# Down-projection products of 512 columns cut into pairs of 256, but for 56 of 240

## The chip, the cores and the metric

The kernel runs on one core of one Trainium2 chip. Its time is the device time of one execution in microseconds, and of several executions the median. TensorE (PE in the profile) does matrix products, VectorE (DVE) and ScalarE (ACT) elementwise work, GpSimd (POOL) odd pieces; SyncE (SP) issues most of the transfers between HBM and SBUF, the memory on the core. PE writes its sums into PSUM, whose banks hold 512 float32 columns each.

## The reference

One decoder layer on 256 tokens of 1024 channels: two mixing branches (a recurrent one and an attention one), merged and projected, and then a gated feed-forward part with a causal convolution of width 3. Only the last part is touched:

```python
def conv_ffn(h, w_up, conv_w, conv_b, w_down):        # h (1, 256, 1024), D_FF = 2816
    u = h @ w_up                                      # (1024, 5632)
    a, b = u[..., :D_FF], u[..., D_FF:]
    a = conv1d_causal(a, conv_w) + conv_b             # width 3, per channel
    return (gelu(a, approximate=False) * b) @ w_down  # (2816, 1024)
...
    x = x + conv_ffn(rms_norm(x, norm2_g), w_ffn_up, ffn_conv_w, ffn_conv_b, w_ffn_down)
```

## The kernel before

All matrix products run in a reduced float32 format. To keep accuracy, each operand is split into a high part and a low remainder (`whi` and `wlo` for weights; `hh`, `hl` and `hb[:, 0]`, `hb[:, 1]` for activations), and each product is done three times: high by high, low by high, high by low.

A product on PE has two operands. The stationary one, 128 by 128, is loaded first by an instruction of its own (PEld in the profile, LDWEIGHTS); then the moving one streams through it, 256 or 512 columns long, and the result is added into PSUM. Every product in this kernel has its own load, also when the tile is the same as before.

Weights come in groups of 1024 columns per partition (512 KB). `weights()` hands out the next group, already split, and has the next ones made ready: ScalarE copies the high part (`split_hi`, line 299), VectorE subtracts for the low part (`split_lo`, line 310), SyncE starts the next transfer (`load_next`). The order of the groups is one fixed queue.

The feed-forward part works in eleven blocks `j` of 256 hidden channels. For each block:

- `up()` computes the gate half into an `acc` bank and then, through `up(atp)`, the value half into an `at` bank. Both run `wst` (lines 346, 348, 351): the weights are stationary, the activations `hx` move, 256 columns (tokens) in each product. That is 2 x 48 = 96 products.
- VectorE and ScalarE scale, convolve and apply GELU, multiply with the value half and split the result into `hb`.
- `down(j, hb)` multiplies with two groups of down-projection weights (`i` = 0, 1), 128 hidden channels each. Here `hb` is stationary and the weights move. There are four sums `fin[f]`, each one bank of 512 columns: `t` is the half of the tokens, `hf` the half of the output channels. Three products each (lines 1464, 1466, 1468) make 2 x 4 x 3 = 24 products of 512 columns.

`down` runs one block behind: block `j`'s down-projection stands on PE after the up-projections of block `j` + 1. The last block's is written out by hand (lines 1513 to 1529): its sums 0 to 2 are done in products of 512 columns, and the last sum in two halves of 256 columns, so that they can be scaled and stored one after another.

Two earlier stages matter for comparison. In `queries` (lines 1322, 1323) one stationary tile serves two products in a row, one of 288 columns into `acc` and one of 256 into `pq`. In the output projection (`xst`, lines 367, 368, 371) `mh` and `ml` are stationary and 512 columns of weights move.

Of the kernel before, what the change touches and what calls it, by code (L numbers as in the profile page):

```python
# [37 lines left out]
def body(tc, x, positions, norm1_g, w_in, rwkv_mu, w_decay_up, decay_bias, w_aaa_up,  # L38
# [3 lines left out]
    act, dve, pool, pe = nc.scalar, nc.vector, nc.gpsimd, nc.tensor  # L42
    ctx = ExitStack()
    with ctx:
# [12 lines left out]
        def b4(name, shape=(128, 4, 256), dt=F32):  # L57
            return sb.tile(list(shape), dt, name=name, tag="b4", bufs=NB4)
# [14 lines left out]
        def chp(name="ch"):  # L73
            return ps.tile([128, 512], F32, name=name, tag="ch", bufs=3)

        def atp(name="at"):
            return ps.tile([128, 512], F32, name=name, tag="at", bufs=2)
# [243 lines left out]
        def weights(n=1):  # L321

            w = ready.pop(0)
            taken[0] += 1
            for _ in range(n):
                with tc.issue_after(fence[0]) if taken[0] < 6 else nullcontext():
                    split_lo()
                    split_hi()
            return w
# [1093 lines left out]
        for i, (c0, c1) in enumerate(zip(WCUT, WCUT[1:])):  # L1423
            cs = slice(c0, c1)
# [31 lines left out]
        def down(j, hb):  # L1456
            for i in range(2):
                wh, wl = weights()
                st = j == 0 and i == 0
                for f in range(4):  # L1460
                    t, hf = divmod(f, 2)
                    ts = slice(t * 128, t * 128 + 128)
                    cs = slice(hf * 512, hf * 512 + 512)
                    pe.matmul(fin[f], hb[:, 0, i, ts], wh[:, 0, cs], start=st, stop=False,  # L1464
                              skip_group_check=f == 3)
                    pe.matmul(fin[f], hb[:, 1, i, ts], wh[:, 0, cs], start=False, stop=False,  # L1466
                              skip_group_check=f == 3)
                    pe.matmul(fin[f], hb[:, 0, i, ts], wl[:, 0, cs], start=False, stop=False,  # L1468
                              skip_group_check=f == 3)

        prev = []
        for j in range(11):
            hb = b4("hb", (128, 2, 2, 256), F32R)
            if j == 0:
# [3 lines left out]
                fin = [chp("f0"), chp("f1"), chp("f2"), atp("f3")]  # L1478
# [5 lines left out]
            for m in range(2):  # L1484
                n = 2 * j + m
# [17 lines left out]
            if len(prev) == 2:  # L1503
                down(*prev.pop(0))
        of = out.rearrange("b s d -> (b s) d")
        j, hb = prev.pop(0)
# [6 lines left out]
        for f, is_ in ((0, (0,)), (1, (0,)), (0, (1,)), (2, (0,)), (1, (1,)), (2, (1,)), (3, (0, 1)), (4, (0, 1))):  # L1513
            t, hf = divmod(min(f, 3), 2)
            ts = slice(t * 128, t * 128 + 128)
            c0, n = ((0, 512), (0, 256), (256, 256))[max(f - 2, 0)]
            fs = last if f == 4 else fin[f][:, c0:c0 + n]
            cs = slice(hf * 512 + c0, hf * 512 + c0 + n)
            kw = dict(skip_group_check=True) if f == 3 else {}
            for i in is_:  # L1520
                wh, wl = ws[i]
# [32 lines left out]
```

## Time and profile before

| | us |
|---|---|
| median of 3 runs | 402.79 (402.75 to 403.62) |
| the profiled execution | 402.01 |
| its span, first to last instruction | 400.2 |
| PE busy in it | 394.3, 99% |
| VectorE busy | 301.9, 75% |
| ScalarE busy | 237.3, 59% |
| one block of the feed-forward part, from the second on | 16.40 |

Times are microseconds from the start of the span unless marked ns. An instruction's group is given by its line, engine, operation, the tile written and the tiles read (`f<-whi,hb` is `fin` from `whi` and `hb`), partitions by columns, and a count. The chain of waits is followed back from the last instruction to what released each step. Products on PE overlap: the end of one lies after the start of the next, so the distance between starts tells what one costs, and the listed duration does not.

### The profile page before, as it was taken

The numbers are of one execution on the slowest core, as the hardware profiler recorded it, in microseconds if no ns is written. First come the engines' busy times: TensorE is split into PE (matmuls) and PEld (weight loads), VectorE is DVE, ScalarE is ACT, GpSimd is POOL, SyncE is SP. The second block draws the span as 40 slices with busy tenths as digits, with TensorE's granted clock in tenths as the row PEclk, the third lists the DMA queues.
The fourth block names the chain that finished last, engine by engine and source line by source line (L and its number), as shares of the span: only waits on it lengthen the run. The fifth ranks groups of instructions, "written<-read, shape, count | busy, mean of one in ns | idle before, by whom it ended". The sixth has DMA issues, their size and how long they took to land.

```text
span 400.2 us, 9024 instructions
## 1 busy us (share of the span) xinstructions
PE 394.3 (99%) x3633; PEld 365.9 (91%) x3633; DVE 301.9 (75%) x508; ACT 237.3 (59%) x411; POOL 49.5 (12%) x87
## 2 busy tenths in 40 slices
PE   8999999999999999999999999999999999999996
PEld 6899999898999989999888999999999999999995
DVE  4989989899868989688875885765757667576583
ACT  5899477494747686635554874554545546455350
POOL 8888000010600021120000000000000000000000
PEclk9999999999999999999999999999999999999999
DMA  8943397554694333555661765666665565665612
GB/s 255 323 147 86 86 305 219 139 153 124 145 292 128 108 98 128 201 162 185 199 195 56 261 206 184 196 189 195 191 208 186 185 208 168 204 211 163 208 52 105
DMA packets 60589, 70.58 MB, mean 176 GB/s; under 512 B 7377, under 2 KB 51287, under 8 KB 60548
## 3 DMA queue, kind: packets, MB, share of 16 engines
q1 hardware_dynamic: 58116, 69.17, 56.1%
q10 hardware_dynamic: 1632, 0.59, 0.6%
q8 instruction: 28, 0.46, 0.5%
q0 software_dynamic: 800, 0.26, 0.4%
q14 instruction: 13, 0.11, 0.1%
HBM read 68.56 MB, written 1.44 MB: 175 GB/s over the span
## 4 chain that ended last, share of the span: by engine, by line
PE 85%; POOL 4%; DMA 4%; DVE 3%; ACT 1%; issue 1%; SPq 0%; POOLq 0%
PE acc L346 11%; PE acc L351 11%; PE acc L348 11%; PE at L351 5%; PE at L346 5%; PE at L348 5%; PE f L1468 5%; PE f L1466 5%; PE f L1464 5%; PE acc L367 4%; PE acc L371 4%; PE acc L368 4%; DMA posi<-in_positions_dram 2%; PE acc L1322 2%; PE pq L1323 1%; DMA p<-in_aaa_bias_dram 1%
## 5 line engine op out<-in xcount | busy, mean ns | idle before, releaser
L299 ACT CAST whi<-raw 128x1024 fp32r<-128x1024 f32 (+1 forms) x122 | 124.5, 1025 | 111.3 <-PE acc L348 44.0
L310 DVE TENSOR_TENSOR wlo<-raw,whi 128x1024 fp32r<-128x1024 f32 (+1 forms) x122 | 144.6, 1188 | 37.7 <-PE f L1468 14.4
L346 PE MATMUL acc<-hx,whi 128*128 128x256 f32 x400 | 99.4, 284 | 0.0
L348 PE MATMUL acc<-hx,whi 128*128 128x256 f32 x400 | 97.1, 279 | 0.0
L346 PEld LDWEIGHTS acc<-hx,whi 128*128 128x128 f32 x400 | 75.4, 188 | 2.4 <-issue 0.8
L348 PEld LDWEIGHTS acc<-hx,whi 128*128 128x128 f32 x400 | 75.4, 188 | 0.4
L351 PE MATMUL acc<-hx,wlo 128*128 128x256 f32 x400 | 62.3, 278 | 0.2 <-DVE rs L1440 0.2
L351 PEld LDWEIGHTS acc<-hx,wlo 128*128 128x128 f32 x400 | 53.2, 188 | 0.4 <-DVE wlo L310 0.4
L346 PE MATMUL at<-hx,whi 128*128 128x256 f32 x176 | 42.4, 278 | 0.0
L348 PE MATMUL at<-hx,whi 128*128 128x256 f32 x176 | 42.3, 277 | 0.0
L348 PEld LDWEIGHTS at<-hx,whi 128*128 128x128 f32 x176 | 33.1, 188 | 0.0
L346 PEld LDWEIGHTS at<-hx,whi 128*128 128x128 f32 x176 | 33.1, 188 | 0.0
L1468 PE MATMUL f<-wlo,hb 128*128 128x512 f32 x80 | 31.6, 395 | 0.0
L1466 PE MATMUL f<-whi,hb 128*128 128x512 f32 x80 | 31.4, 393 | 0.0
L1464 PE MATMUL f<-whi,hb 128*128 128x512 f32 x80 | 31.2, 390 | 0.0
L351 PE MATMUL at<-hx,wlo 128*128 128x256 f32 x176 | 27.3, 277 | 0.0
L351 PEld LDWEIGHTS at<-hx,wlo 128*128 128x128 f32 x176 | 23.3, 188 | 0.0
L1466 PEld LDWEIGHTS f<-whi,hb 128*128 128x128 f32 x80 | 15.0, 188 | 3.1
L1468 PEld LDWEIGHTS f<-wlo,hb 128*128 128x128 f32 x80 | 15.1, 189 | 3.0
L1464 PEld LDWEIGHTS f<-whi,hb 128*128 128x128 f32 x80 | 15.0, 188 | 2.9
L1482 DVE TENSOR_TENSOR an<-acc,rsb 128x512 f32<-128x512 f32 x11 | 7.6, 692 | 13.1 <-PE acc L351 12.9
L1499 DVE TENSOR_TENSOR cv<-cv,at 128x256 f32<-128x256 f32 x22 | 8.3, 417 | 10.2 <-PE at L351 9.9
(359 smaller groups left out, 696.2 us busy)
## 6 DMA issues: line engine op xcount, KB each, us to landing
raw<-in_w_ffn_up_dram SPq DMA_DIRECT2D x44, 512.0 KB, 3.6
raw<-in_w_in_dram SPq DMA_DIRECT2D x33, 512.0 KB, 4.7
raw<-in_w_ffn_down_dram SPq DMA_DIRECT2D x22, 512.0 KB, 3.4
raw<-in_w_out_dram SPq DMA_DIRECT2D x8, 512.0 KB, 4.2
raw<-in_w_in_dram SPq DMA_DIRECT2D x8, 272.0 KB, 2.9
early<-in_w_in_dram SPq DMA_DIRECT2D x2, 1024.0 KB, 8.1
raw<-in_w_branch_b_dram SPq DMA_DIRECT2D x4, 512.0 KB, 3.5
raw<-in_w_branch_a_dram SPq DMA_DIRECT2D x4, 512.0 KB, 3.4
```

The lines of the kernel that those rows point to most:

```text
L299: act.copy(wide(hi, k, c), spread(raw, k, c))
L310: eng.tensor_tensor(wide(lo, k, c), spread(raw, k, c), wide(hi, k, c).bitcast(F32), op=OP.subtract)
L346: pe.matmul(om, wh[:, k, ms], xh[:, k0 + k], start=k0 + k + m == 0, stop=False, skip_group_check=True)
L348: pe.matmul(om, wh[:, k, ms], xl[:, k0 + k], start=False, stop=False, skip_group_check=True)
L351: pe.matmul(om, wl[:, k, ms], xh[:, k0 + k], start=False, stop=k0 + k == nk - 1 and m == n - 1, skip_group_check=True)
L367: pe.matmul(ps_[t], xh[:, K, ts], wh[:, k], start=K == 0, stop=False)
L368: pe.matmul(ps_[t], xl[:, K, ts], wh[:, k], start=False, stop=False)
L371: pe.matmul(ps_[t], xh[:, K, ts], wl[:, k], start=False, stop=K == nk - 1)
L1464: pe.matmul(fin[f], hb[:, 0, i, ts], wh[:, 0, cs], start=st, stop=False, skip_group_check=f == 3)
L1466: pe.matmul(fin[f], hb[:, 1, i, ts], wh[:, 0, cs], start=False, stop=False, skip_group_check=f == 3)
L1468: pe.matmul(fin[f], hb[:, 0, i, ts], wl[:, 0, cs], start=False, stop=False, skip_group_check=f == 3)
L1499: dve.tensor_tensor(cv, cv, pb[:, m], op=OP.mult)
```

## The change

In `down`, the 24 products of a block are numbered `at` = 12 `i` + 3 `f` + `n`, in the order in which they are issued. A list `WIDE` gives for each block how many of the first products keep their 512 columns. Each later one becomes two products of 256 columns, the first and the second half of the same weights into the first and the second half of the same sum, one right after the other, with the same stationary tile. The list is 23 for the first block, 11 for the fourth, seventh and tenth, and 0 for the other six: 56 products stay, 184 become 368.

```diff
-                    cs = slice(hf * 512, hf * 512 + 512)
-                    pe.matmul(fin[f], hb[:, 0, i, ts], wh[:, 0, cs], start=st, stop=False,
-                              skip_group_check=f == 3)
-                    pe.matmul(fin[f], hb[:, 1, i, ts], wh[:, 0, cs], start=False, stop=False,
-                              skip_group_check=f == 3)
-                    pe.matmul(fin[f], hb[:, 0, i, ts], wl[:, 0, cs], start=False, stop=False,
-                              skip_group_check=f == 3)
-
+                    for n, (h, w) in enumerate(((0, wh), (1, wh), (0, wl))):
+
+                        at = 12 * i + 3 * f + n
+                        for c in (0,) if at < WIDE[j] else (0, 256):
+                            e = c + (512 if at < WIDE[j] else 256)
+                            pe.matmul(fin[f][:, c:e], hb[:, h, i, ts], w[:, 0, hf * 512 + c:hf * 512 + e],
+                                      start=st and n == 0 and c == 0, stop=False,
+                                      skip_group_check=f == 3 or at >= WIDE[j])
+
+        WIDE = [23, 0, 0, 11, 0, 0, 11, 0, 0, 11]
         prev = []
```

## Prediction

> **What bounds the kernel now.** I read the page first (span, busy shares, granted clock, the chain that ended last), then the waits in the feed-forward stretch, then busy time block by block, and last the distance between starts of matrix products.
>
> ```profile
> span 400.2 us, 9024 instructions
> PE 394.3 (99%) x3633; PEld 365.9 (91%) x3633; DVE 301.9 (75%) x508; ACT 237.3 (59%) x411; POOL 49.5 (12%) x87
> PEclk9999999999999999999999999999999999999999
> PE 85%; POOL 4%; DMA 4%; DVE 3%; ACT 1%; issue 1%; SPq 0%; POOLq 0%
> PE acc L351 <- DVE rs L1440: 0.2, 1, 0.2
> ```
>
> The matrix engine (PE) is busy for 394.3 of 400.2 us and holds 85% of the chain. The granted clock is full throughout, so no result here can come from the throttle. The fifth line is the whole answer for what PE waited for from 218 us to the end: one wait of 0.2 us. In the feed-forward part nothing is late for PE, and the time is the sum of PE's own starts.
>
> ```profile
> core 0: us, PE busy (x) PEld busy (x) DVE busy (x) ACT busy (x) POOL busy (x), PEclk, DMA share, GB/s
> 218.90:238.10 19.20, 19.18 (x163) 19.01 (x164) 15.86 (x25) 15.74 (x25) 0.00 (x0) 1.00 0.67 221
> 238.10:243.70 5.60, 5.60 (x27) 4.59 (x26) 3.78 (x6) 2.63 (x4) 0.00 (x0) 1.00 0.60 194
> 243.70:260.10 16.40, 16.40 (x122) 15.42 (x121) 10.78 (x15) 8.70 (x12) 0.00 (x0) 1.00 0.62 193
> 374.90:391.30 16.40, 16.40 (x122) 15.42 (x121) 10.78 (x15) 7.65 (x11) 0.00 (x0) 1.00 0.28 95
> ```
>
> Nine stretches of 16.40 us from 243.70 to 391.30 (first and last shown) each hold one block's up-projection, 96 products of 256 columns, and the previous block's down-projection, 24 products of 512 columns. PE is busy in all 16.40; VectorE in 10.78, ScalarE in 8.70. A product's listed duration overlaps its neighbours', so what a product costs is read from start to start. The next rows are single starts (start, duration, line).
>
> ```profile
> 245.19 0.28 PE L346 MATMUL acc<-hx,whi 128*128 128x256 f32 x1
> 254.71 0.39 PE L1464 MATMUL f<-whi,hb 128*128 128x512 f32 x1
> 260.20 0.28 PE L346 MATMUL acc<-hx,whi 128*128 128x256 f32 x1
> 260.80 0.28 PE L348 MATMUL acc<-hx,whi 128*128 128x256 f32 x1
> ```
>
> From 245.19 to 254.71 there are 84 products of 256: 9.52/84 = 113.3 ns each. From 254.71 to 260.20 there are the 24 of 512: 5.49/24 = 228.8 ns each. Two of 256 would take 226.7. So 512 columns in one product cost here 2.1 ns more than twice 256: that is all there is to gain from a pair. The first five starts after the wide ones, 260.20 to 260.80, take 0.600 us where five at the usual pace take 0.567: 0.033 us of excess where the down-projection hands over to the up-projection. 84 + 24 products and the hand-over account for the 16.40 us (96 x 113.3 + 5.49 + 0.03 = 16.40).
>
> The pace was not always that. The first block ran slower:
>
> ```profile
> 233.66 0.47 PE at L351 x4
> 237.90 0.47 PE at L351 x4
> 238.21 0.40 PE L1464 MATMUL f<-whi,hb 128*128 128x512 f32 x1
> 243.81 0.28 PE L346 MATMUL acc<-hx,whi 128*128 128x256 f32 x1
> ```
>
> The first two rows (chain in order of time) lie 36 products apart: 4.24/36 = 117.8 ns for 256 columns. The other two are 24 wide ones apart: 5.60/24 = 233.3 ns. Both kinds are 4.5 ns slower than later, at the same clock and with no wait: a slow pace that outlives the change from 256 to 512 columns and has ended by 245.19, a dozen products after the change back (the 84 above). At this pace a pair costs 235.6, 2.3 ns more than one wide product. I name no cause; the forecast turns on which pace the pairs run at.
>
> **The change, part by part.** Of 240 products of 512 columns in blocks 0 to 9, 23 + 11 + 11 + 11 = 56 stay wide. The other 184 become pairs: 1 in block 0, 24 in each of blocks 1, 2, 4, 5, 7, 8 (144), 13 in each of blocks 3, 6, 9 (39). Order, operands, weights and accumulators stay; each pair loads its stationary hb tile twice. That adds 184 products and 184 loads to 3633 of each. The eleventh block is untouched.
>
> Pairs in blocks 1 to 9: 183 pairs. Is 113.3 the right price with hb stationary and half a weight row moving? The rows that are nearest are the kernel's own last products, which have exactly this shape:
>
> ```profile
> 395.53 0.28 PE L1522 MATMUL f<-whi,hb 128*128 128x256 f32 x1
> 396.77 0.28 PE L1524 MATMUL acc<-wlo,hb 128*128 128x256 f32 x1
> ```
>
> Eleven steps in 1.24 us, 112.7 ns at a resolution of 0.9: the fast pace. They differ from the pairs in one thing, each has its own stationary tile. The other near row has that thing, and is worse. In the query projection each stationary tile serves a product of 288 and then one of 256 columns:
>
> ```profile
> 50.25 0.29 PE L1322 MATMUL acc<-wlo,hx 128*128 128x288 f32 x1
> 53.25 0.29 PE L1322 MATMUL acc<-wlo,hx 128*128 128x288 f32 x1
> ```
>
> Twelve such pairs in 3.00 us, 250.0 each, where 544 columns at 113.3 per 256 would take 240.8: 9.2 more, the slow pace twice over (2 x 4.5). So the ends for a pair of 256 are 226.7 and 235.9, against 228.8 for a wide one: -0.38 us and +1.30 us for 183. I take 226.7, since the last products have the width, the operands and the line of PSUM of the pairs, and the blocks around them have run at that pace for 147 us; 288 columns occur nowhere in the change.
>
> The one pair of block 0: it comes at the slow pace, +0.002 us. Nothing.
>
> The hand-over excess of 0.033 us: it could vanish in the six blocks that have no wide product left (-0.20 us) or stay. In the last block wide products are followed by 256s with the same operands, and those run at once at 113 (the rows from 395.53), so the excess seems to belong to the change of operands, which stays. I take 0; the ends are -0.20 and 0. In blocks 3, 6 and 9 a change of width moves into the middle of the down-projection: 0 by the same rows, +0.033 each (0.10) at worst.
>
> Loads: in the down-projection the load of 188 ns has 229 ns of wide product to hide in; with 256 it has 113.
>
> ```profile
> L1464 PEld LDWEIGHTS f<-whi,hb 128*128 128x128 f32 x80 | 15.0, 188 | 2.9
> L346 PEld LDWEIGHTS acc<-hx,whi 128*128 128x128 f32 x400 | 75.4, 188 | 2.4 <-issue 0.8
> q8 instruction: 28, 0.46, 0.5%
> q8 instruction: 8, 0.13, 0.4%
> ```
>
> The up-projection has the same 188 ns in front of every 113.3-ns product, so the listed load, too, overlaps, and its 113.3 already holds whatever a load costs. Should that cover go (a load waiting for the end of the product before it), the price is that of the query pairs above.
>
> Program: 368 more instructions beside 7266 of these two kinds is 5% of 0.46 MB, one or two more fetches beside 28. Eight of the 28 fall into the nine stretches (the last row is the same view for 244 to 391 us), which do not differ; cost 0, and a fetch costs at most the 0.01 us by which those stretches could differ.
>
> Waits, queues, buffers: no transfer or other engine's instruction is added or moved. The first product of a pair holds the waits of the wide one; PE's 0.08 us per block shorter supply time leaves VectorE's 10.78 of 16.3 us and ScalarE's 8.70 as cover. Cost 0; if the weights came late, the first to show it would be a load's wait for wlo.
>
> Sum: 183 x -2.1 = -0.38 us. The profiled execution took 402.01 us (400.2 span and 1.8 around it), so 401.6; the median of the three runs, 402.79, lies 0.78 above that, and on its scale the forecast is 402.4. Three runs spread over 0.87 us, so about 0.2% (0.8 us) is what a measurement of this kernel can tell from no change: I forecast a gain that is too small to be told.
>
> [...]
>
> **The rivals.**
>
> *A fixed cost per product, or no gain at all.* At the slow pace doubling the number of products costs 2.3 ns each; in the output projection 512 columns took
>
> ```profile
> 205.37 0.47 PE acc L371 x2
> 212.18 0.45 PE acc L371 x2
> ```
>
> 6.81/30 = 227.0 ns, no worse than two of 256. So the 2.1 ns may come from what the down-projection's operands do to each other, which a pair would keep. Then the change gives between 0 and 183 x 2.3 = +0.42 us: 402.8 to 403.2. Against it: the last rows at 113. [...]
>
> *The other side: pairs on one stationary tile run at the slow pace.* For it: the query pairs never reached the fast pace in the rows shown. 183 x (235.6 to 235.9 - 228.8) = +1.24 to +1.30 us, 404.1. It decides from 233.2 ns per pair on (0.8 us/183 = 4.4 above 228.8). Worse, the slow pace outlived a change of width in block 0, so it could run on into the next up-projection: 96 x 4.5 = 0.43 us per block, up to 3.9 for nine, 404.5 to 408. Against that stands what follows the query pairs:
>
> ```profile
> 54.25 0.28 PE L346 MATMUL acc<-hx,whi 128*128 128x256 f32 x1
> 55.18 0.61 PE L351 MATMUL acc<-hx,wlo 128*128 128x256 f32 x4
> 55.63 0.28 PE L346 MATMUL acc<-hx,whi 128*128 128x256 f32 x1
> ```
>
> The first eight products take 0.93 us (116 each), the next four 0.45 (112.5): the pace becomes fast within a dozen products, as after block 0.
>
> *A larger gain.* Two loads of the same tile might overlap better than two different ones. To pass 0.8 us with the hand-over gone (-0.20) a pair must take 225.5; with it kept, 224.4. No row shows 256 columns in 112.2, but none shows equal pairs of 256 either. 400.9 to 402.0.
>
> **How the numbers follow.** Forecast (pairs at 113.3, 402.0 to 402.6) 0.50. No gain or a fixed cost (402.6 to 403.4) 0.14. Slow pairs alone (403.8 to 404.6) 0.13; slow pace carried on (404.6 to 408) 0.07. Larger gain 0.16. The point is the forecast's 402.4. The range 401.4 to 404.6 leaves out the carried case and the lower part of the larger gain, some 0.13. The likeliest case's own range is 402.0 to 402.6. Faster by over 0.2%: 0.16; within: 0.50 + 0.14 = 0.64; slower: 0.20.
>
> **What would show it.** Right: stretches of about 16.32 to 16.37 us in place of 16.40 for blocks 1 to 9, starts 113.3 ns apart inside the down-projections, block 0 unchanged at 233.3, PE's products and loads at 3817 each, no new wait. Wrong: starts at 117 to 120 in the pairs; up-projections of blocks 2 to 10 over 10.9 us; stretches that differ between fully and partly paired blocks by more than 0.05 us; or a load waiting where none waited before.

## The result

The changed kernel takes 405.36 us (median of five runs, 404.74 to 405.98); the kernel before, in five runs beside it, 403.34 (402.75 to 403.62). The ratio is 1.0057, with a 95% interval of 1.0041 to 1.0073: slower by 0.4 to 0.7% (2.0 us between the medians, 2.3 between the means), and above the range that was given (401.4 to 404.6).

The page of the changed kernel, in the lines that answer to those of before: span, busy shares, granted clock, instruction fetches, chain.

```profile
span 403.6 us, 9392 instructions
PE 397.8 (99%) x3817; PEld 376.3 (93%) x3817; DVE 302.0 (75%) x508; ACT 237.5 (59%) x411; POOL 48.0 (12%) x87
PEclk9999999999999999999999999999999999999999
q8 instruction: 30, 0.49, 0.5%
PE 91%; DVE 4%; ACT 2%; issue 1%; POOL 1%; DVEq 0%; ACTq 0%
```

And all that PE waited for from 218 us to the end (who, for whom, us in total, times, longest):

```profile
PE acc L351 <- DVE wlo L310: 0.2, 1, 0.2
```

Nothing of note has changed in these lines. PE is busy all the time at full clock, the other engines do what they did, and the single wait is as short as before; it stands at 219.5 us, ahead of the edited code, and the kernel before shows the same line in its second profile (e5). PE has 3.5 us more of busy time: its products take longer. Which ones is seen when the stretches are cut at the hand-overs, from the first product of one projection to the first of the next (window, its length, busy us of PE and of its loads with counts, then the other engines).

```profile
238.84:244.44 5.60, 5.60 (x28) 4.59 (x26) 3.79 (x6) 2.55 (x5) 0.00 (x0) 1.00 0.70 204
244.44:255.74 11.30, 11.30 (x98) 11.30 (x97) 6.99 (x9) 6.17 (x9) 0.00 (x0) 1.00 0.60 182
255.74:261.40 5.66, 5.66 (x50) 5.66 (x49) 3.78 (x6) 2.56 (x5) 0.00 (x0) 1.00 0.68 205
261.40:272.29 10.89, 10.89 (x98) 10.89 (x97) 6.99 (x9) 6.15 (x9) 0.00 (x0) 1.00 0.59 184
272.29:277.73 5.44, 5.44 (x50) 5.44 (x49) 3.79 (x6) 2.55 (x5) 0.00 (x0) 1.00 0.63 205
277.73:289.04 11.31, 11.31 (x98) 11.31 (x97) 6.99 (x9) 6.16 (x9) 0.00 (x0) 1.00 0.59 182
289.04:294.68 5.64, 5.64 (x40) 5.16 (x39) 3.79 (x6) 2.56 (x5) 0.00 (x0) 1.00 0.65 198
294.68:305.57 10.89, 10.89 (x98) 10.89 (x97) 6.99 (x9) 6.15 (x9) 0.00 (x0) 1.00 0.59 188
```

Rows take turns: down-projection of the first block, up-projection, down-projection of the second, and so on. The up-projections are the same 96 products as before, in the same order. Before, each of them took 10.90 or 10.91 us behind the first down-projection. Here they take 11.30, 10.89, 11.31, 10.89: 117.8 or 113.4 ns per product, the two paces of the prediction. Five of the nine that follow a changed down-projection are slow, 5 x 0.40 = +2.0 us; all five stand where nothing was edited. The down-projections themselves take 5.66 us in three of the six blocks that are all pairs and 5.44 in the other three, and 5.58 to 5.64 in the three mixed ones, against 5.49 for wide products at the fast pace: +0.69 us over all. The four fast up-projections give back 0.015 us each. Together 2.65 us of the 3.4 by which the spans differ. Of the rest, 0.63 lies ahead: the first down-projection starts at 238.84 and not at 238.21, behind code that is the same in both. Another 0.1 lies in the last block. (The two profiled executions are farther apart than the medians, since the one of the kernel before, 402.01, lies 1.3 us below the median of its runs.)

The pace also turns inside a down-projection. The seventh block enters behind a fast up-projection; these are its eleven wide products and then its thirteen pairs:

```profile
338.87:341.39 2.52, 2.52 (x14) 2.07 (x12) 2.25 (x5) 1.47 (x3) 0.00 (x0) 1.00 0.72 208
341.39:344.45 3.06, 3.06 (x28) 3.06 (x26) 1.54 (x2) 1.08 (x2) 0.00 (x0) 1.00 0.63 196
```

The wide ones take 228.8 ns each, the fast pace; the 26 products behind them take 117.7, the slow one, from the first of them on. The next up-projection is slow, too (11.31 us).

So the change put about half of the feed-forward part on the slow pace. The experiments ask what sets the pace.

### The profile page after: what moved, and what is told of

Its sections match the earlier page's. It is cut to its first block, busy times and chain, and to the rows that moved or that the text cites. A ratio compares the mean times of both kernels' runs of the same rounds, so it can differ in the third digit from the quotient of the medians.

```text
span 403.6 us, 9392 instructions
## 1 busy us (share of the span) xinstructions
PE 397.8 (99%) x3817; PEld 376.3 (93%) x3817; DVE 302.0 (75%) x508; ACT 237.5 (59%) x411; POOL 48.0 (12%) x87
## 4 chain that ended last, share of the span: by engine, by line
PE 91%; DVE 4%; ACT 2%; issue 1%; POOL 1%; DVEq 0%; ACTq 0%
PE f L1468 14%; PE acc L346 13%; PE acc L351 12%; PE acc L348 12%; PE at L346 5%; PE at L351 5%; PE at L348 5%; PE acc L367 4%; PE acc L371 4%; PE acc L368 4%; PE acc L1322 1%; PE pq L1323 1%; PE pgr L773 1%; PE acc L498 1%; PE idle L115 1%
## 5 line engine op out<-in xcount | busy, mean ns | idle before, releaser
L1468 PE MATMUL f<-whi,hb 128*128 128x256 f32 (+1 forms) x280 | 50.2, 295 | 0.0
L346 PE MATMUL at<-hx,whi 128*128 128x256 f32 x176 | 43.1, 280 | 0.0
L348 PE MATMUL at<-hx,whi 128*128 128x256 f32 x176 | 43.0, 280 | 0.0
L1468 PEld LDWEIGHTS f<-whi,hb 128*128 128x128 f32 x280 | 39.5, 188 | 1.4
L1468 PE MATMUL f<-wlo,hb 128*128 128x256 f32 (+1 forms) x144 | 31.6, 292 | 0.0
L1468 PEld LDWEIGHTS f<-wlo,hb 128*128 128x128 f32 x144 | 22.8, 188 | 1.0
L1029 POOL TENSOR_TENSOR st<-st,mhalf 128x4 f32<-128x4 f32 x4 | 5.9, 1474 | 59.2 <-DVE mx L1201 30.9
L367 PE MATMUL acc<-whi,hx 128*128 128x512 f32 x32 | 12.8, 399 | 0.0
```

The costliest lines, as they stand in the source:

```text
L346: pe.matmul(om, wh[:, k, ms], xh[:, k0 + k], start=k0 + k + m == 0, stop=False, skip_group_check=True)
L348: pe.matmul(om, wh[:, k, ms], xl[:, k0 + k], start=False, stop=False, skip_group_check=True)
L367: pe.matmul(ps_[t], xh[:, K, ts], wh[:, k], start=K == 0, stop=False)
L1029: pool.tensor_tensor(st[:, 2], st[:, 1], mhalf, op=OP.pow)
L1468: pe.matmul(fin[f][:, c:e], hb[:, h, i, ts], w[:, 0, hf * 512 + c:hf * 512 + e], start=st and n == 0 and c == 0, stop=False, skip_group_ch ...
```

## The experiments

Two theories stood first. H: the pace is a state that PE carries along and that only a hand-over from a down- to an up-projection can change, in a way that depends on whether wide products or pairs stand before it. S: two loads of one stationary tile in a row are slow, as the query projection seemed to show.

**e1: pairs in the third block alone**

```diff
-        WIDE = [23, 0, 0, 11, 0, 0, 11, 0, 0, 11]
+        WIDE = [24, 24, 0, 24, 24, 24, 24, 24, 24, 24]
```

> Only the third block's 24 products are pairs; all others keep 512 columns. Theory H (PE has two paces for these products, 113.3 and 117.8 ns per 256 columns; it keeps the one that it has, and only a hand-over from a down-projection to the next up-projection can change it: after wide products it comes out fast, after pairs it flips): the third block enters fast and its pairs take 5.44 us; the next up-projection is slow, 11.31 us in place of 10.91; the fourth block's wide products take 5.60 in place of 5.49; the up-projection after them is fast again, 10.90. In all +0.45 us over 16.40 us blocks. Theory S (two loads of the same stationary tile in a row slow the pair): the pairs take 5.66 us and every up-projection 10.91: +0.16 us, none of it outside the third block. [...]

One timed run, 404.84 us. The windows from the first down-projection to the fifth:

```profile
238.70:244.22 5.52, 5.52 (x27) 4.52 (x26) 3.78 (x6) 2.55 (x5) 0.00 (x0) 1.00 0.70 204
244.22:255.52 11.30, 11.30 (x97) 11.30 (x96) 6.99 (x9) 6.17 (x9) 0.00 (x0) 1.00 0.58 182
255.52:261.04 5.52, 5.52 (x27) 4.52 (x26) 3.78 (x6) 2.55 (x5) 0.00 (x0) 1.00 0.69 202
261.04:272.34 11.30, 11.30 (x97) 11.30 (x96) 6.99 (x9) 6.16 (x9) 0.00 (x0) 1.00 0.58 181
272.34:277.99 5.65, 5.65 (x50) 5.65 (x49) 3.78 (x6) 2.56 (x5) 0.00 (x0) 1.00 0.66 195
277.99:289.30 11.31, 11.31 (x98) 11.31 (x97) 6.99 (x9) 6.16 (x9) 0.00 (x0) 1.00 0.57 184
289.30:294.90 5.60, 5.60 (x26) 4.55 (x25) 3.78 (x6) 2.55 (x5) 0.00 (x0) 1.00 0.66 202
294.90:305.80 10.90, 10.90 (x97) 10.90 (x96) 6.99 (x9) 6.16 (x9) 0.00 (x0) 1.00 0.59 185
305.80:311.30 5.50, 5.50 (x27) 4.52 (x26) 3.78 (x6) 2.56 (x5) 0.00 (x0) 1.00 0.66 202
```

H was half wrong. Up to 272 us this program is the kernel before, and yet its wide products took 5.52 us (neither 5.60 nor 5.49) and both up-projections behind them were slow. So wide products do not always hand over to the fast pace, and an execution can come into the feed-forward part in a way of its own. Three phases have been seen so far, told apart by what a down-projection of wide products takes: fast (5.49), a slow one that wide products keep (5.51 to 5.52), and a slow one that they turn into the fast one (5.60). The pairs of the third block led out of the second into the third; the fourth block's wide products took 5.60, and from 294.90 on all was fast to the end. S, too, forecast fast up-projections, and two were slow with no pair ahead of them; its price for the pairs, 5.66, is near the 5.65 that they took, and e3 has to decide there.

Here the phase can't be read from the products just before the hand-over. The second down-projection, cut behind its fifth product:

```profile
255.52:256.69 1.17, 1.17 (x7) 0.95 (x6) 0.90 (x3) 1.17 (x3) 0.00 (x0) 1.00 0.65 135
256.69:261.04 4.35, 4.35 (x21) 3.57 (x20) 2.89 (x4) 1.38 (x3) 0.00 (x0) 1.00 0.71 220
```

Five products take 233 ns each and the other nineteen 229, the fast pace, and yet the up-projection behind them is slow (11.30 us).

**e2 and e3: nine blocks of pairs, in order and taken apart**

e2 has the first block wide and all others in pairs (`WIDE = [24, 0, 0, 0, 0, 0, 0, 0, 0, 0]`). e3 has the same products, in an order in which no tile is loaded twice in a row:

```diff
+                if not WIDE[j]:
+                    order = [(f, n, c) for fs in ((0, 2), (1, 3)) for n in range(3) for c in (0, 256) for f in fs]
```

> First block all wide, the other nine all pairs. H: the pace alternates. First block slow and wide, then up fast (10.90 us), pairs fast (5.44), up slow (11.31), pairs slow (5.66), up fast, and so on: four slow up-projections x 0.40, four slow sets of pairs x 0.16, five fast ones x -0.05: about +2.0 us on the kernel before, a ratio of 1.005. S: all nine sets of pairs at 5.66 and all up-projections at 10.90: +1.5 us, with no alternation. [...]

> As the one before (first block wide, nine blocks all products of 256), but the order of a group's products is changed so that two sums with different token halves take turns: no stationary tile is loaded twice in a row. H: as without this, alternating up-projections of 10.90 and 11.31 us, about +2.0 us. S: no product is slowed, 5.44 us for each down-projection and 10.90 for each up-projection: -0.4 to -0.6 us.

e2: 405.70 us, ratio to the kernel before 1.0033 (0.9997 to 1.0068). e3: 405.11, ratio 1.0004 (0.9970 to 1.0039). The times alone decide nothing; the windows do. Both executions came in at the lasting slow phase: their first down-projection took 5.51 us and the first two up-projections 11.31 each, where H had the first one fast. What follows is e2 from the second of these on, and then four windows of e3:

```profile
261.95:273.26 11.31, 11.31 (x99) 11.31 (x98) 6.99 (x9) 6.16 (x9) 0.00 (x0) 1.00 0.56 179
273.26:278.91 5.65, 5.65 (x50) 5.65 (x49) 3.78 (x6) 2.54 (x5) 0.00 (x0) 1.00 0.65 196
278.91:289.80 10.89, 10.89 (x98) 10.89 (x97) 6.99 (x9) 6.15 (x9) 0.00 (x0) 1.00 0.60 188
289.80:295.25 5.45, 5.45 (x51) 5.45 (x49) 3.78 (x6) 2.56 (x5) 0.00 (x0) 1.00 0.64 201
295.25:306.56 11.31, 11.31 (x99) 11.31 (x98) 6.99 (x9) 6.17 (x9) 0.00 (x0) 1.00 0.58 183
306.56:312.21 5.65, 5.65 (x50) 5.65 (x49) 3.78 (x6) 2.54 (x5) 0.00 (x0) 1.00 0.67 199
```

```profile
278.19:289.08 10.89, 10.89 (x98) 10.89 (x97) 6.99 (x9) 5.92 (x9) 0.00 (x0) 1.00 0.61 188
289.08:294.52 5.44, 5.44 (x50) 5.44 (x49) 3.78 (x6) 2.77 (x5) 0.00 (x0) 1.00 0.66 201
294.52:305.84 11.32, 11.32 (x99) 11.32 (x98) 6.99 (x9) 5.95 (x9) 0.00 (x0) 1.00 0.58 183
305.84:311.49 5.65, 5.65 (x50) 5.65 (x49) 3.78 (x6) 2.78 (x5) 0.00 (x0) 1.00 0.60 198
```

From there both alternate to the end: fast, slow, fast, slow. A pair costs 226.7 ns at the fast pace and 235.7 at the slow one, whether its two loads are the same tile or not. S is out. Fast pairs (5.44 us) are followed by a slow up-projection (11.31) and slow pairs (5.65) by a fast one (10.89), as in the six blocks of the changed kernel that are all pairs.

**e4: the last three products of each block wide**

```diff
+                        wide = at < WIDE[j] or at >= 21
```

> First block all wide; in the other nine blocks the first 21 products are pairs and the last three keep 512 columns, so that wide products stand before each up-projection. H: every up-projection is fast (10.91 us), the down-projections take 5.45: 9 x -0.04 = -0.4 us on the kernel before, a ratio of 0.999, hardly to be told from it, and 2.5 us faster than the changed kernel. S: pairs at 235.6, 9 x 21 x 6.8 ns = +1.3 us. [...]

402.93 us, ratio 0.9968 (0.9921 to 1.0014): no difference that can be told. In its profile all nine such down-projections, and the up-projections behind the first eight, read like these two lines:

```profile
255.42:260.86 5.44, 5.44 (x47) 5.33 (x46) 3.78 (x6) 2.54 (x5) 0.00 (x0) 1.00 0.61 200
260.86:271.77 10.91, 10.91 (x97) 10.90 (x96) 6.99 (x9) 6.17 (x9) 0.00 (x0) 1.00 0.60 190
```

21 pairs, and no flip: with wide products at the end of a fast down-projection the next up-projection stays fast (10.91 us), with 21 pairs ahead of them as with none in the kernel before. The interval is wide since the kernel before, beside these kernels, took 402.09 to 407.75 in its 29 runs and this kernel 401.75 to 409.50. A phase that an execution keeps to the end would spread them so (nine slow up-projections are 3.6 us), but no such run was profiled, and this stays an argument.

**e5 and e7: the kernel before again, and one pair**

e5 is the kernel before. e7 changes one product of it, the last of the third block (`WIDE = [24, 24, 23, 24, ...]`).

> The kernel before, unchanged, profiled once more. Theory P (the pace is a phase that an execution brings into the first block and that each hand-over maps to the next: wide products keep fast as fast and one slow phase as slow): either all up-projections from the second block on take 10.91 us and the down-projections 5.49, or all take 11.31 and 5.51 (4.2 us more), never a mixture after the second block. Rival M (the pace is drawn anew by chance at every hand-over): a mixture of 10.9 and 11.3. Rival N (the kernel before is always fast, slow paces come from pairs alone): 10.91 throughout.

> The kernel before, with only the very last product of the third block's down-projection as a pair. P, if the execution is fast there: the next up-projection takes 11.31 us, the fourth block's wide products 5.60, and all after it is fast again: +0.5 us for one pair. If it comes in at the lasting slow phase: the next up-projection is slow, too, and it shows which phase follows. A theory by which each pair costs its own price: +0.007 us at most, no other stretch changed.

e5 took 402.06 us, and its windows are those of the kernel before: 5.60, then 10.90 and 5.49 to the end. That fits P and N alike; the sequence of e1 is against N. e7 took 402.90 us:

```profile
260.58:271.49 10.91, 10.91 (x98) 10.91 (x96) 6.99 (x9) 6.16 (x9) 0.00 (x0) 1.00 0.60 191
271.49:276.99 5.50, 5.50 (x28) 4.56 (x26) 3.78 (x6) 2.56 (x5) 0.00 (x0) 1.00 0.69 205
276.99:288.29 11.30, 11.30 (x98) 11.30 (x97) 6.99 (x9) 6.16 (x9) 0.00 (x0) 1.00 0.58 181
288.29:293.89 5.60, 5.60 (x26) 4.54 (x25) 3.78 (x6) 2.55 (x5) 0.00 (x0) 1.00 0.71 195
293.89:304.79 10.90, 10.90 (x97) 10.90 (x96) 6.99 (x9) 6.16 (x9) 0.00 (x0) 1.00 0.59 190
```

One pair in 240 products: its own block is 0.01 us longer, the next up-projection 0.40, the next wide products 0.11, and then all is as before. The two halves of the pair took 120 and 119 ns from start to start, behind wide products of 228.8: as in the seventh block of the changed kernel, the pace turns with the first product of 256, and the up-projection goes on at it. This is the clearest run: the price sits behind the hand-over and is fifty times the price of the pair.

**e6 and e8: leaving the slow phase on purpose**

e6: first block wide, second all pairs, third wide, later ones 21 pairs and three wide products. e8: second block pairs, all others wide.

> First block wide, second block all pairs, third block all wide; from the fourth block on the first 21 products are pairs and the last three wide. P: pairs send both the fast and the lasting slow phase to a slow phase that the wide products of the third block turn into the fast one: whatever pace comes in, every up-projection after the third block takes 10.91 us and each later down-projection 5.45. One slow up-projection (0.40) and slower wide products (0.11) are paid, 7 x 0.05 us come back: 402 to 403.5 us in every execution, none in the upper group of the kernel before (405 to 408). M or N: executions in the upper group as often as with the kernel before.

> First block wide, second all pairs, all others wide. P: as with the reset before, every up-projection after the third block 10.91 us and every later down-projection 5.49: 402.3 to 404 us in every execution, none in the upper group of the kernel before; against the fast executions of the kernel before +0.5 us, against its slow ones -3.5. M or N: the upper group as often as with the kernel before.

e6: 403.11 us (402.46 to 404.85), ratio 1.0000 (0.9987 to 1.0014). e8: 403.69 (402.52 to 405.23), ratio 1.0005 (0.9991 to 1.0020). Two of e6's twelve runs lie above the 403.5 us that were expected at most, and four of e8's above 404. These runs were on another chip than those of e1 to e4; the kernel before took 402.06 to 404.48 beside them and had no upper group, so the timed runs do not test whether a reset protects from one. The profile of e6 does show a reset at work: it came in at the lasting slow phase.

```profile
238.91:244.43 5.52, 5.52 (x27) 4.51 (x26) 3.79 (x6) 2.55 (x5) 0.00 (x0) 1.00 0.69 201
244.43:255.73 11.30, 11.30 (x97) 11.30 (x96) 6.99 (x9) 6.16 (x9) 0.00 (x0) 1.00 0.56 182
255.73:261.38 5.65, 5.65 (x50) 5.65 (x49) 3.79 (x6) 2.55 (x5) 0.00 (x0) 1.00 0.62 196
261.38:272.69 11.31, 11.31 (x98) 11.31 (x97) 6.99 (x9) 6.16 (x9) 0.00 (x0) 1.00 0.58 185
272.69:278.29 5.60, 5.60 (x26) 4.54 (x25) 3.78 (x6) 2.55 (x5) 0.00 (x0) 1.00 0.67 196
278.29:289.19 10.90, 10.90 (x97) 10.90 (x96) 6.99 (x9) 6.16 (x9) 0.00 (x0) 1.00 0.57 189
```

Pairs, then wide products, and it is fast from 278.29 to the end, as in e1. e8 came in as the kernel before does, went slow behind its pairs and fast behind the next wide products. Both paths are those that P gave; a pace drawn by chance at each hand-over would hardly alternate as it does in e2 and e3 from the fourth block to the end, or stay fast as it does in e1, e5, e7 and e8. Neither kernel is shown to be faster than the kernel before.

**e9: the activations moved by some bytes**

The last question was what the pace is. `hx`, which streams through PE in every up-projection, starts 48 columns into its tile. On top of e2 only that start was changed, in both of the lines that name the tile (one shown), so the earlier products that stream `hx` moved with it:

```diff
-        hx = cst.tile([128, 4144], F32R, name="hx", tag="hx")[:, 48:4144]
+        hx = cst.tile([128, 4144], F32R, name="hx", tag="hx")[:, 0:4096]
```

> The kernel with nine blocks of pairs (e2), but the activations hx lie 192 bytes lower in each partition (they start at column 0 of their tile and not at 48); nothing else moves. Theory O (order and lengths alone): down- and up-projections take the values of e2, 5.44 and 5.66 us, 10.89 and 11.31, and alternate in the same way from the fourth block on. Theory A (place in memory): other times of an up-projection than these two, or another sequence.

> As e2, with hx 128 bytes lower. O: the values and the alternation of e2. A: other times or another sequence, and not the same as with 192 bytes.

> As e2, with hx 64 bytes lower. O: the values and the alternation of e2. A: other times or another sequence.

> As e2, with hx 16 bytes lower. O: the values and the alternation of e2. A: other times or another sequence, if 16 bytes are enough to matter.

One run each: 409.90, 409.13, 409.27 and 410.91 us for starts at column 0, 16, 32 and 44, with the kernel before at 402.63 beside them. One up-projection of each, in that order (the fourth behind the first down-projection):

```profile
297.53:309.05 11.52, 11.52 (x99) 11.52 (x97) 6.99 (x9) 6.17 (x9) 0.00 (x0) 1.00 0.55 179
```

```profile
296.70:308.01 11.31, 11.31 (x99) 11.31 (x98) 6.98 (x9) 6.17 (x9) 0.00 (x0) 1.00 0.56 180
```

```profile
296.36:307.75 11.39, 11.39 (x99) 11.39 (x97) 6.98 (x9) 6.16 (x9) 0.00 (x0) 1.00 0.58 181
```

```profile
297.63:309.08 11.45, 11.45 (x99) 11.45 (x97) 6.99 (x9) 6.17 (x9) 0.00 (x0) 1.00 0.60 179
```

Theory O falls. With the same instructions in the same order, 120.0, 117.8, 118.7 and 119.3 ns per product in place of 113.4 or 117.8; the alternation is gone from the fourth block on, and no up-projection behind the first down-projection is fast in any of the four. Even 16 bytes change both values and sequence. So order and lengths alone don't set the paces: where the streamed operand lies in memory has a part in it. One execution of each place was profiled, so the phases that a place has are not all known. A start at 48 is not the only one with a fast phase, either. The last 129 products of 256 ahead of the first down-projection, with the start at 16 and then in e2, with the start at 48:

```profile
225.70:240.32 14.62, 14.62 (x131) 14.62 (x130) 12.76 (x20) 11.85 (x20) 0.00 (x0) 1.00 0.76 239
224.28:239.47 15.19, 15.19 (x131) 15.19 (x130) 12.85 (x20) 11.77 (x20) 0.00 (x0) 1.00 0.73 234
```

With 16 they ran at 113.3 ns each, with 48 at 117.8. What in the memory or on the way to PE makes it so isn't shown by these runs.

## Why the prediction was wrong

Right were the frame and the small things: no new wait, no clock, no supply from the other engines (PE's waits, the clock row and VectorE's 10.8 us per block are as before); two more fetches for the longer program, 30 for 28, and no wait of PE for them; 3817 products and loads; the first block unchanged at 5.60; and the price of a pair at the fast pace, 226.7 ns, which the fast blocks show (5.44 us for 24).

The step that failed is the hand-over. The prediction took it as 0, with ends of -0.20 and 0 us in all, because its excess of 0.033 us was all that the trace before showed there. A hand-over was priced as a cost of its own, where it decides the pace of the next 96 products: 0.40 us each time that it comes out slow, +2.02 us for the five. The first of the five stands behind the one pair of block 0, which the prediction put at nothing: 11.30 us, where the kernel before takes 10.90. And the change of width inside a down-projection, put at 0 by the kernel's last products, turned the seventh block (block 6) from the fast pace to the slow one. Some of the material was at hand. The first block showed that a slow pace lasts across projections, and the prediction noted it and priced a slow pace that pairs hand on (404.6 to 408, with a chance of 0.07). The measured 405.36 lies in there, but by another mechanism, so that is luck: in the six blocks that are all pairs, fast pairs (5.44) were followed by a slow up-projection and slow ones (5.66) by a fast one. The prediction set that chance low on two cases in which a slow stretch had ended within a dozen products. Both were cases of leaving the slow pace; neither showed a pair before a hand-over out of the fast one, which is what the change makes.

The second step that was off is the price of a pair. One value was taken for all 183, -2.1 ns; the pairs ran at both paces, and the nine down-projections came to +0.69 us in place of -0.38 (some 0.1 of it from wide products on the slow pace). The nearest rows, the kernel's last products, gave the fast pace only because PE happened to be fast there. In the changed kernel the same products, unedited, read:

```profile
398.82 0.28 PE L1524 MATMUL f<-whi,hb 128*128 128x256 f32 x1
400.12 0.28 PE L1526 MATMUL acc<-wlo,hb 128*128 128x256 f32 x1
```

Eleven steps in 1.30 us are 118 ns each, the slow pace, and the sixteen wide products ahead of them took 228.9 ns. The other rows, the query pairs, were read as a hint that two loads of one tile are slow; e3 shows that in the down-projection they are not.

The rival of a fixed cost for each added product, at the 2.3 ns that the slow pace of the trace before gave, would have made +0.42 us, spread evenly over the pairs. The sign is right, but e7's +0.5 us for one pair, and e4 with 189 pairs and no slower stretch (5.44 us for a down-projection, 10.91 for an up-projection), show that it isn't what happened.

## What to carry to other kernels

When an engine is busy all the time and the question is a few ns per instruction, look at the start-to-start distance of the same instruction over the whole trace first: if it has two values at one clock, an edit can move whole stretches between them, and that can outweigh what the edit saves (here 0.40 us for each up-projection that turned slow, against 0.05 us for a down-projection of fast pairs). Judge such an edit by the stretches that it leaves alone, and change what stands just before a hand-over one instruction at a time. Take no price for an instruction from one stretch of one execution. The start of an operand in memory is a size to be tried like any other: 192 bytes were worth up to 0.6 us per up-projection here.

## What the runs showed of the hardware

- Matrix products of one shape, back to back at full clock and with no wait, ran at 113.4 and at 117.8 ns per 256 columns in one program; PE kept a pace over the 96 products of an up-projection (10.89 or 11.31 us) and turned at a change of operands (from pairs in 5.44 us to an up-projection in 11.31) or of width (from 228.8 ns for 512 columns to 117.7 for 256, in the seventh block); behind one pair in place of a wide product, ahead of a change of operands, the next 96 products took 11.30 us, where the kernel before takes 10.90 or 10.91 (e7).
- The same code came into the feed-forward part in more than one phase: 5.60 us for the first down-projection in the kernel before, the changed one, e4, e5, e7 and e8, and 5.51 to 5.52 in e1, e2, e3 and e6.
- Moving the streamed operand by 16 to 192 bytes changed a product by up to 6.6 ns (113.4 in e2, 120.0 in e9 with the start at column 0; one execution of each place). The runs show only that the place of the streamed operand matters to the pace, and they leave open why.
